# Moving the gate sigmoids of an output tile to a later step, and cutting the last tile's final steps into halves

## The chip, the cores and the metric

The kernel runs on one core of one Trainium2 chip. The metric is the device time of one launch in microseconds (us). A core has five instruction streams that run in order, each by itself, and meet only at semaphores: TensorE (PE in the profile, with its weight loads under PEld), VectorE (DVE), ScalarE (ACT), GpSimd (POOL) and SyncE (SP), which here only issues DMA transfers. Sixteen DMA engines move the data between HBM and SBUF.

## The reference

The program computes one layer of a streaming encoder for 2048 new frames of one stream and for 16 frames of each of 8 running streams (the sample, 128 rows in all, with caches of 512 past frames each). With width 1024, per row:

```
h        = rms_norm(x) * (1 + scale) + shift                 # scale, shift, gate from c @ w_ada + b_ada
qa ka va za qb kb vb zb ga gb = split(h @ w_in)              # 4 x 512, 4 x 512, 2 x 1024 columns
oa       = (softmax1 - lam * softmax2) @ va                  # differential attention, 4 heads
ob       = stick_breaking(qb, kb) @ vb                       # 8 heads
ya       = (rms_norm(oa) * silu(za)) @ w_branch_a
yb       = (ob * silu(zb)) @ w_branch_b
x        = x + gate * ((sigmoid(ga) * ya + sigmoid(gb) * yb) @ w_out)
y        = rms_norm(x) * final_g
```

The outputs are y for all rows and the keys and values ka, va, kb, vb of all new rows. The change lies in the last four lines: in where sigmoid(ga) and sigmoid(gb) are computed, and in the last addition, the norm and the store of y for one of the tiles.

## The kernel before

Rows are worked in 17 tiles of 128: 16 tiles of the prompt (0 to 15) and one for the sample (16). Float32 accuracy comes from float16 matmuls on a high part and a low part of each operand, so every product is three matmuls, and each operand is cut into two halves by a scaled copy (ACT, line 290) and a subtraction (DVE, line 295).

The phases before the last write to HBM, for every tile, the attention results (o_d), the z columns (z_d) and the 2048 gate columns before their sigmoid (g_d). The last phase, lines 1255 on, turns these into y. Two streams of work share it.

The first stream goes through the tiles in the order 0 to 14, 16, 15 (the list `tiles`); the very last is thus tile 15 of the prompt, and the sample is the one before it. A tile passes through these steps:

- `inputs(t)`, lines 1144 to 1179: SP loads o, z and two gate buffers of 128 x 1024 (line 1152); ACT takes the sigmoid of z, DVE and POOL form u = o * silu(z); then two ACT instructions take the sigmoid of the gate buffers in place (line 1167, recorded at line 119, the helper `act`); u is squared and summed (line 272), scaled and split (290, 295).
- `turned(st)`: PE transposes the two halves of u (line 1141) and ACT copies each result out of PSUM (line 1142).
- `branches(st)`: four groups of 12 matmuls (line 1289), each followed on DVE by a product with a gate (line 1291), a sum (1294) and the split into y16 (1295 on ACT, 1296 on DVE).
- `turned_y(st)`: the same transposes and copies for y (lines 1141, 1142).
- `output(t, st, box)`: loads x (line 1311), two groups of 24 matmuls (line 1318), each followed by a product with the adaLN gate (line 1322 on DVE for the prompt, lines 1324 and 1325 for the sample) and the addition to x on POOL (line 1326).
- `normed_rows(t, box)`: squares of x (ACT, line 272), the reciprocal root (ten tiny DVE instructions, lines 253 to 264), the scaling (line 1334) and the store (line 1335).

In round n the loop emits the branches of the n-th tile, the inputs of tile n + 2, the transposing of u of tile n + 1, the norm of tile n - 2, the output of tile n - 1 and the transposing of y of the n-th tile. Four gate buffers serve two tiles at a time, so the gates of tile n + 2 can be loaded only when the branches of tile n have used the buffers (line 1296 or 1291 on DVE).

The second stream is the attention of the sample rows against the caches, in eight units, spread over the first 13 rounds: cache loads (line 728), their cuts (k16c, v16c at lines 290 and 295), transposes made by the DMA engines (lines 735 and 570), scores (line 753), softmax or stick-breaking with sigmoids and exponentials through `act`, and products with the values (line 784, copied out at line 787).

Within a round the pieces are sorted by their share of the round's cost (`interleave`). The order on each engine is then fixed at compile time by a scheduler that goes by its own estimate of durations and readiness. One constraint is written by hand: all instructions made with `act` (sigmoids and exponentials) keep the order in which the program emits them, since a change between the two functions costs a table load on ACT.

Of the kernel before, what the change touches and what calls it, by code (L numbers as in the profile page):

```python
# [16 lines left out]
F32 = mybir.dt.float32  # L17
# [3 lines left out]
AF = mybir.ActivationFunctionType  # L21
ALU = mybir.AluOpType
# [3 lines left out]
P = 128  # L26
D = 1024
# [82 lines left out]
def layer_kernel(ctx: ExitStack, tc: tile.TileContext, a: dict):  # L110
    nc = tc.nc
    V, S, G, T = nc.vector, nc.scalar, nc.gpsimd, nc.tensor
    load = nc.sync.dma_start
# [3 lines left out]
    def act(**kw):  # L117

        i = S.activation(**kw)  # L119
        if last_table[0] is not None:  # L120
            tc.add_manual_dep(i.ins, last_table[0].ins.name, NOSYNC, reason="table order")
        last_table[0] = i
        return i
# [30 lines left out]
    def y_rows(t):  # L154
        return y_p[t * P : (t + 1) * P, :] if t < NT else y_s
# [92 lines left out]
    def rsqrt_one(sums, width, pool, name):  # L248

        c = tiny.tile([P, 4], F32, tag="r1", name="r1")  # L250
        q, t, w = c[:, 0:1], c[:, 1:2], c[:, 2:3]
        i = c[:, 3:4].bitcast(I32)
        V.tensor_scalar(out=q, in0=sums, scalar1=1.0 / width, scalar2=EPS, op0=ALU.mult, op1=ALU.add)
        V.tensor_scalar(out=i, in0=q.bitcast(I32), scalar1=1, scalar2=None, op0=ALU.logical_shift_right)
        y = pool.tile([P, 1], I32, tag=name, name=name)
        V.tensor_scalar(out=y, in0=i, scalar1=-1.0, scalar2=1597463007.0, op0=ALU.mult, op1=ALU.add)
        y = y.bitcast(F32)
        V.scalar_tensor_tensor(out=t, in0=y, scalar=y, in1=q, op0=ALU.mult, op1=ALU.mult)
        V.tensor_scalar(out=w, in0=t, scalar1=0.375, scalar2=-1.25, op0=ALU.mult, op1=ALU.add)
        V.tensor_scalar(out=w, in0=w, scalar1=t, scalar2=1.875, op0=ALU.mult, op1=ALU.add)  # L260
        V.tensor_tensor(out=y, in0=y, in1=w, op=ALU.mult)
        V.scalar_tensor_tensor(out=t, in0=y, scalar=y, in1=q, op0=ALU.mult, op1=ALU.mult)
        V.tensor_scalar(out=w, in0=t, scalar1=-0.5, scalar2=1.5, op0=ALU.mult, op1=ALU.add)
        V.tensor_tensor(out=y, in0=y, in1=w, op=ALU.mult)
        return y

    def sum_squares(src, n, dst, width=1024, scale=1.0):

        for i in range(0, n, width):
            junk = tiny.tile([P, width], F16, tag="junk", name="junk", bufs=1)  # L270
            w = min(width, n - i)
            S.activation(out=junk[:, 0:w], in_=src[:, i : i + w], func=AF.Square, scale=scale,
                         accum_out=dst[:, i // width : i // width + 1])
# [870 lines left out]
    def inputs(t):  # L1144

        o, z = hs[0:2]
        load(out=o, in_=o_d[t])
        load(out=z, in_=z_d[t])
        gs = []
        for j in range(2):  # L1150
            gs.append(L["g"][(2 * len(begun) + j) % 4].rearrange("p (b n) -> p b n", b=2))
            load(out=gs[j], in_=g_d[t].rearrange("p (b n) -> p b n", b=2)[:, :, j * 512 : (j + 1) * 512])
        begun.append(t)
        r = L["orms"][:, 4 * t : 4 * t + 4] if t < NT else rsqrt(osums[:, NT, :], 4, P, tiny, "rA")
        for n in range(2):
            c = slice(n * 512, (n + 1) * 512)
            sg = bank("mm")
            act(out=sg, in_=z[:, c], func=AF.Sigmoid)
            G.tensor_tensor(out=o[:, c], in0=o[:, c], in1=z[:, c], op=ALU.mult)
            if n == 1:  # L1160
                V.tensor_tensor(out=o[:, c], in0=o[:, c], in1=sg, op=ALU.mult)
            else:
                for h in range(4):
                    c = slice(h * P, (h + 1) * P)
                    V.scalar_tensor_tensor(out=o[:, c], in0=sg[:, c], scalar=r[:, h : h + 1], in1=o[:, c], op0=ALU.mult, op1=ALU.mult)
        for g in gs:
            act(out=g, in_=g, func=AF.Sigmoid)

        sq = tiny.tile([P, 2], F32, tag="usq", name="usq")
        sum_squares(o, D, sq[:, 0:1])  # L1170
        V.tensor_tensor(out=sq[:, 1:2], in0=sq[:, 0:1], in1=L["wsq"], op=ALU.mult)
        sc = scales(sq, unit, "suy", 2)
        u16 = hs[2].bitcast(F16).rearrange("p (f n) -> p f n", f=2)
        split(u16[:, 0, :], u16[:, 1, :], o, sc[:, 0:1], S)

        f = unit.tile([P, 2], F32, tag="fuy", name="fuy", bufs=4)
        V.tensor_scalar(out=f[:, 0:1], in0=sc[:, 2:3], scalar1=sc[:, 1:2], scalar2=L["s"][0][:, 1:2], op0=ALU.mult, op1=ALU.mult)
        V.tensor_tensor(out=f[:, 1:2], in0=sc[:, 3:4], in1=L["s"][1][:, 1:2], op=ALU.mult)
        return dict(u16=u16, u=L["u"][len(begun) % 2], f=f, g=gs)

    def turned(st):

        st["u"] = st["u"].bitcast(F16).rearrange("p (k n) -> p k n", n=P)
        for half in range(2):
            transposed(st["u16"], st["u"], half)
# [69 lines left out]
    with ExitStack() as c2:  # L1255
# [50 lines left out]
        def output(t, st, box):  # L1306

            def half(j):
                if j == 0:
                    box["x"] = s2.tile([P, D], F32, tag="x", name="x2", bufs=2)  # L1310
                    load(out=box["x"], in_=x_rows(t))
                x = box["x"]
                c = slice(j * 512, (j + 1) * 512)
                po = bank("o")
                n = 0
                for yi, wi in ((0, 0), (0, 1), (1, 0)):
                    for k in range(KT):
                        T.matmul(po, st["y"][:, yi * 8 + k, :], wo[j * 4 + k // 2][:, wi, k % 2, :], start=(n == 0), stop=(n == 3 * KT - 1))  # L1318
                        n += 1
                m = s2.tile([P, 512], F32, tag="sg", name="m", bufs=2)  # L1320
                if t < NT:
                    V.scalar_tensor_tensor(out=m, in0=po, scalar=st["f"][:, 1:2], in1=gate[:, c], op0=ALU.mult, op1=ALU.mult)
                else:
                    S.activation(out=m, in_=po, func=AF.Identity, scale=st["f"][:, 1:2])
                    V.tensor_tensor(out=m, in0=m, in1=gate_rows(1, j), op=ALU.mult)
                G.tensor_tensor(out=x[:, c], in0=m, in1=x[:, c], op=ALU.add)
            return [(5.2, lambda j=j: half(j)) for j in range(2)]

        def normed_rows(t, box):
            x = box["x"]  # L1330
            acc = tiny.tile([P, 1], F32, tag="facc", name="facc")
            sum_squares(x, D, acc)
            r = rsqrt_one(acc, D, tiny, "rF")
            V.scalar_tensor_tensor(out=x, in0=x, scalar=r, in1=fg, op0=ALU.mult, op1=ALU.mult)
            load(out=y_rows(t), in_=x)

        qpad = res.tile([P, 4, NB, 32], F16, name="qpad")
        G.memset(qpad, 0.0)
# [62 lines left out]
```

## Time and profile before

| what | value |
|---|---|
| time, median of 3 runs | 2353.01 us (2352.11 to 2354.78) |
| time of the profiled execution | 2352.26 us |
| span of the profiled execution | 2350.5 us |
| mean granted TensorE clock | 0.965 of full speed |
| busy: PE / DVE / ACT / POOL | 2124.5 / 1729.8 / 1635.9 / 687.0 us |
| DMA transfers | 453.74 MB, mean 193 GB/s |
| first matmul of the last phase's branches (line 1289) | 1824.06 us |

The profiled execution took 1.8 us more than its span, and 0.75 us less than the median of the timed runs. A line of a timeline gives the start, the duration, the engine, the line of the kernel, the operation, output <- input, and in square brackets the idle time of that engine just before with what ended it. Names of buffers are reused: wb and wa are 128 x 1024 buffers that hold gates, u, y or weights in this phase.

### The profile page before, as it was taken

What the parts mean: (1) busy time and instruction counts of PE and PEld (TensorE: products, weight loads), DVE (VectorE), ACT (ScalarE), POOL (GpSimd) and SP (SyncE); (2) the same over time, 40 slices, a digit from 0 to 9 for tenths busy, and PEclk for the clock granted to TensorE, in tenths of its full rate; (3) what the DMA queues carried; (4) which work ended last, traced back from release to release, by engine and by line L of the source; (5) the groups of instructions that cost most, each with busy time, mean ns of one, the idle gap of its engine ahead of it and who ended that gap; (6) DMA issues with size and microseconds to landing.
All of it is one profiled execution on the core that took longest, in us unless ns stands there. A gap on an engine that the chain in (4) does not pass through costs nothing. (4 is left out here: it accounts for less than half of the span.)

```text
span 2350.5 us, 42534 instructions
## 1 busy us (share of the span) xinstructions
PE 2124.5 (90%) x15272; PEld 1147.0 (49%) x15272; DVE 1729.8 (74%) x3604; ACT 1635.9 (70%) x3148; POOL 687.0 (29%) x563
## 2 busy tenths in 40 slices
PE   5898898998999899899999989999995789889998
PEld 3554454444555444445554544555553344445453
DVE  4847865779775567988666798867678777878763
ACT  4557777777786777778677787866677666666541
POOL 1533012345310233632023364203334222222221
PEclk8999999999999999999999999999997899999999
DMA  9766669887795898878678796866677999998621
GB/s 336 254 203 175 158 137 252 196 195 158 188 238 134 192 222 195 174 171 197 137 178 204 170 196 171 203 150 162 151 170 166 290 254 255 282 238 239 178 100 55
DMA packets 843572, 453.74 MB, mean 193 GB/s; under 512 B 538234, under 2 KB 786346, under 8 KB 842848
## 3 DMA queue, kind: packets, MB, share of 16 engines
q1 hardware_dynamic: 842412, 450.63, 77.2%
q8 instruction: 119, 1.95, 0.3%
q14 instruction: 93, 0.76, 0.1%
q10 hardware_dynamic: 948, 0.39, 0.1%
HBM read 249.80 MB, written 73.44 MB: 138 GB/s over the span
## 5 line engine op out<-in xcount | busy, mean ns | idle before, releaser
L612 POOL TENSOR_TENSOR sc_p<-sc_p,sc_n 128x127 f32<-128x127 f32 (+7 forms) x192 | 311.3, 1625 | 885.5 <-DVE sc_n L606 870.5
L427 PE MATMUL ps_mm<-wb,hs 128*128 128x512 f16 x1632 | 413.4, 380 | 5.0 <-DMA hs<-hT_d 3.2
L427 PEld LDWEIGHTS <-hs 128*128 128x128 f16 x3120 | 273.8, 99 | 252.3 <-issue 12.5
L427 PE MATMUL ps_mm<-wa,hs 128*128 128x512 f16 x1488 | 378.4, 385 | 3.4 <-DVE v L295 2.4
L606 DVE TENSOR_TENSOR_SCAN sc_n<-ps_s,sc_n,zero_t 128x512 f32<-128x512 f32 x192 | 245.3, 1278 | 75.6 <-ACT ps_s L119 72.5
L629 PE MATMUL ps_s<-k,qst 128*128 128x512 f16 (+3 forms) x640 | 225.7, 354 | 47.2 <-DVE sc_n L606 33.7
L563 DVE TENSOR_TENSOR sc_n<-sc_p,sc_n 128x128 f16<-128x128 f32 (+7 forms) x192 | 219.9, 1150 | 51.3 <-ACT sc_n L562 50.8
L494 PEld LDWEIGHTS <-hs 128*128 128x128 f16 x1632 | 154.8, 98 | 182.9 <-DVE qst L522 7.8
L119 ACT ACTIVATE sc_p<-ps_s,usc 128x512 f32<-128x512 f32 (+3 forms) x320 | 203.7, 636 | 44.9 <-PE ps_s L630 34.7
L630 PE MATMUL ps_s<-k,qst 128*128 128x512 f16 (+3 forms) x640 | 225.6, 354 | 0.0
L681 PE MATMUL ps_o<-v,wt 128*128 128x128 f16 x1088 | 175.3, 226 | 36.3 <-DMA wt<-sc_n 36.2
L562 ACT CAST sc_n<-sc_p 128x128 f16<-128x128 f32 (+7 forms) x192 | 154.5, 808 | 65.7 <-POOL sc_p L612 65.0
L494 PE MATMUL ps_t<-wb,hs 128*128 128x512 f16 x816 | 193.5, 381 | 7.0 <-DVE qst L522 6.9
L119 ACT ACTIVATE ps_s<-ps_s,usc 128x512 f32<-128x512 f32 (+3 forms) x328 | 198.6, 606 | 0.0
L494 PE MATMUL ps_t<-wa,hs 128*128 128x512 f16 x816 | 192.1, 380 | 1.7 <-ACT qst L522 1.7
L1318 PE MATMUL ps_o<-wo,wb 128*128 128x512 f16 x816 | 188.6, 386 | 0.7 <-ACT wb L1142 0.7
L682 PE MATMUL ps_o<-v,wt 128*128 128x64 f16 x1088 | 160.1, 198 | 0.0
L681 PEld LDWEIGHTS <-wt 128*128 128x128 f16 x1088 | 106.3, 102 | 104.6 <-DMA wt<-sc_n 48.2
L606 DVE TENSOR_TENSOR_SCAN sc_n<-ps_s,zero_t 128x128 f32<-128x128 f32 (+3 forms) x128 | 104.3, 815 | 48.4 <-ACT ps_s L119 46.3
L548 DVE TENSOR_SCALAR_CACHE_REDUCE sc_p<-ps_s,usc 128x512 f32<-128x512 f32 (+3 forms) x160 | 106.1, 664 | 42.3 <-PE ps_s L630 27.2
L682 PEld LDWEIGHTS <-wt 128*128 128x128 f16 x1088 | 103.9, 101 | 56.3 <-issue 1.9
L548 DVE TENSOR_SCALAR_CACHE_REDUCE sc_n<-ps_s,usc 128x512 f32<-128x512 f32 (+3 forms) x160 | 106.2, 664 | 31.5 <-PE ps_s L630 13.7
(345 smaller groups left out, 4478.0 us busy)
## 6 DMA issues: line engine op xcount, KB each, us to landing
hs<-hT_d SPq DMA_DIRECT2D x130, 512.0 KB, 4.5
g_d<-gt SPq DMA_DIRECT2D x68, 256.0 KB, 4.2
wb<-g_d SPq DMA_DIRECT2D x26, 512.0 KB, 5.7
out_dram<-pr SPq DMA_DIRECT2D x204, 64.0 KB, 2.1
z_d<-pr SPq DMA_DIRECT2D x136, 64.0 KB, 1.8
o_d<-o SPq DMA_DIRECT2D x136, 64.0 KB, 2.4
hs<-z_d SPq DMA_DIRECT2D x17, 512.0 KB, 5.0
hs<-o_d SPq DMA_DIRECT2D x17, 512.0 KB, 6.4
```

Source lines behind the costliest of these rows:

```text
L119: i = S.activation(**kw)
L427: T.matmul(box["p"], box["h"][:, hi, k, :], U["w"][k][:, wi, :], start=(n == 0), stop=(n == 3 * KT - 1))
L494: T.matmul(box["g"][:, 0:gw], box["h"][:, hi, k, :], U["wg"][k // per][:, k % per, wi, :], start=(j == 0), stop=(j == 3 * KT - 1))
L548: V.tensor_scalar(out=dst[:, lo : lo + n], in0=p[:, 0:n], scalar1=sc_pos, scalar2=None, op0=ALU.mult, op1=ALU.max, accum_out=job["mx"][:, ...
L563: V.tensor_tensor(out=lo, in0=src, in1=hi, op=ALU.subtract)
L606: V.tensor_tensor_scan(out=dst[:, lo : lo + n][:, ::-1], data0=src[:, 0:n][:, ::-1], data1=zero_t[:, 0:1].to_broadcast([P, n]), initial=fi ...
L612: G.tensor_tensor(out=p[:, 0:m], in0=p[:, 0:m], in1=n[:, 1 : m + 1], op=ALU.mult)
L629: T.matmul(p[:, 0:n], qst[:, c, :], kk[:, c, 0:n], start=True, stop=False)
L630: T.matmul(p[:, 0:n], qst[:, 2 + c, :], kk[:, c, 0:n], start=False, stop=not diag)
L681: T.matmul(po[:, c * P : (c + 1) * P], wt[:, wj, :], vt[:, c, :, :], start=first, stop=False)
L682: T.matmul(po[:, c * P : c * P + 64], wt[:, nb + wj, :], vt[:, c, 0, :], start=False, stop=last)
L1318: T.matmul(po, st["y"][:, yi * 8 + k, :], wo[j * 4 + k // 2][:, wi, k % 2, :], start=(n == 0), stop=(n == 3 * KT - 1))
```

## The change

Two things. First, the two gate sigmoids leave the end of the first half of `inputs` and are emitted at the beginning of `turned`, for the same tile. For the tiles that the main loop prepares this is one round later: `inputs` of tile n + 2 is emitted in round n, `turned` of that tile in round n + 1. Second, for the last tile alone, the two additions to x go to DVE instead of POOL; the squares are summed in two halves of 512 columns into two columns of `acc`, which a DVE reduction (`add_up`, line 279) adds; and scaling and store are done for columns 0 to 511 and then for 512 to 1023, with two stores of 256 KB instead of one of 512 KB.

```diff
@@ inputs
-        for g in gs:
-            act(out=g, in_=g, func=AF.Sigmoid)
@@ turned
+        for g in st["g"]:
+            act(out=g, in_=g, func=AF.Sigmoid)
         st["u"] = st["u"].bitcast(F16).rearrange("p (k n) -> p k n", n=P)
         for half in range(2):
             transposed(st["u16"], st["u"], half)
@@ output
-                G.tensor_tensor(out=x[:, c], in0=m, in1=x[:, c], op=ALU.add)
+                (V if t == tiles[-1] else G).tensor_tensor(out=x[:, c], in0=m, in1=x[:, c], op=ALU.add)
@@ normed_rows
+            if t != tiles[-1]:
                 acc = tiny.tile([P, 1], F32, tag="facc", name="facc")
                 sum_squares(x, D, acc)
                 r = rsqrt_one(acc, D, tiny, "rF")
                 V.scalar_tensor_tensor(out=x, in0=x, scalar=r, in1=fg, op0=ALU.mult, op1=ALU.mult)
                 load(out=y_rows(t), in_=x)
+                return
+
+            acc = tiny.tile([P, 2], F32, tag="usq", name="usq")
+            sum_squares(x, D, acc, 512)
+            r = rsqrt_one(add_up(acc, 2), D, tiny, "rF")
+            for j in range(2):
+                c = slice(j * 512, (j + 1) * 512)
+                V.scalar_tensor_tensor(out=x[:, c], in0=x[:, c], scalar=r, in1=fg[:, c], op0=ALU.mult, op1=ALU.mult)
+                load(out=y_rows(t)[:, c], in_=x[:, c])
```

More of the change, by code (lines that the diff above doesn't have):

```diff
@@ L1330, in normed_rows @@
             x = box["x"]
[L1331 to L1335, printed above, removed]
+            if t != tiles[-1]:
+                acc = tiny.tile([P, 1], F32, tag="facc", name="facc")
+                sum_squares(x, D, acc)
+                r = rsqrt_one(acc, D, tiny, "rF")
+                V.scalar_tensor_tensor(out=x, in0=x, scalar=r, in1=fg, op0=ALU.mult, op1=ALU.mult)
+                load(out=y_rows(t), in_=x)
+                return
[6 more added lines that the diff above has]
+                load(out=y_rows(t)[:, c], in_=x[:, c])
         qpad = res.tile([P, 4, NB, 32], F16, name="qpad")
```

## The prediction, made before the changed kernel ran

> **What bounds the kernel now.** I read the chain that ended last, then busy time by stage, then what ACT waits for in the stage that the change touches. The chain by line, as shares of the whole span:
>
> ```profile
> PE ps_o L1318 3%; PE ps_mm L1289 2%; DMA wb<-g_d 1%; DMA dwt<-dsc 0%; DVE v16c L295 0%; DMA dc<-in_cache_a_k_dram 0%; PE ps_s L1141 0%; DMA dks<-k16c 0%; PE ps_t L784 0%; ACT v16c L290 0%; DVE wb L1291 0%; DMA dc<-in_cache_b_v_dram 0%; DMA dc<-in_cache_b_k_dram 0%; DMA wa<-g_d 0%; DVE wa L1296 0%
> ```
>
> Its two largest parts are matmuls of the last phase, the third the wait for a gate load (g_d), which only the gate sigmoids have. Next, the last phase in four stages. Columns after the window: PE, PEld, DVE, ACT and POOL busy us with instruction counts, granted clock, DMA share, GB/s.
>
> ```profile
> 1860.00:2210.00 350.00, 313.77 (x2731) 163.43 (x2729) 277.91 (x569) 234.11 (x335) 79.56 (x52) 0.96 0.97 253
> 2210.00:2340.00 130.00, 129.26 (x817) 63.72 (x815) 69.57 (x159) 50.12 (x70) 21.91 (x17) 0.98 0.24 84
> 2340.00:2351.00 11.00, 0.11 (x1) 0.00 (x0) 6.27 (x17) 1.15 (x2) 1.26 (x1) 0.72 0.23 95
> ```
>
> From 2210 to 2340 PE is busy 129.26 of 130.00 us: its order alone sets the length, and what ACT does there is worth nothing. From 1860 to 2210 nothing is full but DMA (0.97): PE has 350 - 313.8 = 36.2 us free. After 2340 a tail of small steps runs out. So the first part of the change can pay only in the middle stage, the second only in the tail. In the middle stage ACT waits for (us in all, times, longest):
>
> ```profile
> ACT wb L119 <- DMA wb<-g_d: 26.7, 13, 4.9
> ACT k16c L290 <- DMA dc<-in_cache_a_k_dram: 17.6, 10, 3.8
> ACT k16c L290 <- DMA dc<-in_cache_b_k_dram: 13.5, 9, 3.3
> ```
>
> The gate sigmoids are the largest group, but casts that wait for the caches (17.6 + 13.5 = 31.1 us) stand in the same queue.
>
> **Part 1: the sigmoids move.** Nothing is added or removed: 34 sigmoids of 1.06 us, the table loads and all g_d loads stay. Emission is a round later, but the scheduler decides the order. In the compiled order on ACT, of the sigmoids of the middle stage that waited, these eight now stand later, behind work that is ready:
>
> ```profile
> 1956.88 1.06 ACT L119 ACTIVATE wb<-wb 128x1024 f32<-128x1024 f32 x1 [3.04 <-DMA wb<-g_d]
> 1979.89 1.06 ACT L119 ACTIVATE wb<-wb 128x1024 f32<-128x1024 f32 x1 [0.38 <-DMA wb<-g_d]
> 1988.29 1.06 ACT L119 ACTIVATE wb<-wb 128x1024 f32<-128x1024 f32 x1 [3.10 <-DMA wb<-g_d]
> 2039.54 1.06 ACT L119 ACTIVATE wb<-wb 128x1024 f32<-128x1024 f32 x1 [1.38 <-DMA wb<-g_d]
> 2051.37 1.06 ACT L119 ACTIVATE wb<-wb 128x1024 f32<-128x1024 f32 x1 [0.27 <-DMA wb<-g_d]
> 2072.22 1.06 ACT L119 ACTIVATE wa<-wa 128x1024 f32<-128x1024 f32 x1 [0.24 <-DMA wa<-g_d]
> 2086.16 1.06 ACT L119 ACTIVATE wb<-wb 128x1024 f32<-128x1024 f32 x1 [2.32 <-DMA wb<-g_d]
> 2145.48 1.06 ACT L119 ACTIVATE wb<-wb 128x1024 f32<-128x1024 f32 x1 [3.03 <-DMA wb<-g_d]
> ```
>
> Their waits add up to 3.04 + 0.38 + 3.10 + 1.38 + 0.27 + 0.24 + 2.32 + 3.03 = 13.8 us. Four others keep their neighbours, and with them their waits (first and last of the four):
>
> ```profile
> 2105.50 1.06 ACT L119 ACTIVATE wb<-wb 128x1024 f32<-128x1024 f32 x1 [1.10 <-DMA wb<-g_d]
> 2179.96 1.06 ACT L119 ACTIVATE wb<-wb 128x1024 f32<-128x1024 f32 x1 [4.86 <-DMA wb<-g_d]
> ```
>
> So the change does half of what its words say: about 13 us of gate waits stay. From 2190 on the ACT order is the old one but for neighbours that swap. The loads themselves are released by DVE at the same points, and no DMA is moved by hand; on SP the compiled order differs by a place or two.
>
> What ACT gains counts only where PE stands still for it. These are PE's gaps that the moved instructions, or the order that comes with them, can touch, and the pace of the matmuls behind a gap and elsewhere:
>
> ```profile
> 1991.28 0.40 PE L753 MATMUL ps_s<-dks,qpad 128*32 128x512 f16 x3 [1.93 <-ACT o L658]
> 1994.71 1.91 PE L1289 MATMUL ps_mm<-wa,wb 128*128 128x512 f16 x4
> 2015.58 0.61 PE L1141 MATMUL ps_s<-id,wa 128*128 128x128 f16 x8 [2.14 <-ACT wa L1142]
> 2044.38 0.48 PE L796 MATMUL ps_t<-ident,ot 128*128 128x128 f32 x1 [4.06 <-ACT ot L787]
> 2046.19 5.91 PE L1318 MATMUL ps_o<-wo,wb 128*128 128x512 f16 x23
> 2052.02 1.05 PE L753 MATMUL ps_s<-dks,qpad 128*32 128x512 f16 x16
> 2044.79 1.47 PE L753 MATMUL ps_s<-dks,qpad 128*32 128x512 f16 x12
> 2080.73 0.74 PE L784 MATMUL ps_t<-dwt,v16c 128*128 128x16 f16 x24 [2.66 <-ACT ot L787]
> 2108.70 0.52 PE L784 MATMUL ps_t<-dwt,v16c 128*64 128x16 f16 x12 [1.86 <-DMA dwt<-dsc]
> 2111.84 1.67 PE L784 MATMUL ps_t<-dwt,v16c 128*64 128x16 f16 x36 [2.10 <-DMA dwt<-dsc]
> 2207.47 0.52 PE L784 MATMUL ps_t<-dwt,v16c 128*64 128x16 f16 x12 [3.24 <-DMA dwt<-dsc]
> 2224.30 5.29 PE ps_o L1318 x24
> ```
>
> - 2044.38: PE waits 4.06 us for `ot`. Ahead of it on ACT stood the sigmoid at 2039.54, with 1.38 of waiting and 1.06 of work; it now stands behind `ot`. Gain 2.4.
> - 2080.73: of the 2.66, the sigmoid at 2072.22 (0.24 + 1.06) stood ahead of the square that feeds u. Gain 1.3.
> - 1991.28: the sigmoid at 1988.29 stood ahead, but so does a cast of a cache, which itself had to wait for its DMA. Nothing gained.
> - 2015.58: a loss. In the new order two sigmoids more stand in the full stretch of ACT ahead of the copy that PE waits for (one square leaves the stretch and one cast enters it, which I let cancel): 2 x 1.06 = 2.1 lost.
> - 2108.70 and 2111.84 (3.96 together) and 2207.47 (3.24): waits for transposed scores. The new PE order puts nine output matmuls more in front of the first two and four branch matmuls more in front of the last: at 5.29 / 24 = 0.22 us each, 2.0 and 0.9 of these gaps would be filled.
> - Slow clock: behind the gap of 4.06, 23 matmuls take 5.91 and twelve of line 753 take 1.47; at the pace of 2224.30 and 2052.02 that would be 5.07 and 0.79, so the gap cost another 1.5.
>
> The last three sums, 2.0 + 0.9 + 1.5 = 4.4, hang on order and clock rather than on a step that I can follow, and I take half, 2.2. The Trainium skill (TensorE: Matmul & The Clock Gate, "What's actually happening") says that the clock halves after an idle window of about 3.4 us; by that, a gap cut from 4.06 to 1.7 would cost no clock, and the whole 1.5 would come back. The trace does not bear it out: behind the gap of 1.93 at 1991.28, four matmuls take 1.91 against 4 x 0.22, twice the usual time, so short gaps lose the clock too.
>
> Middle stage: -2.4 - 1.3 + 2.1 - 2.2 = -3.8 us. Bounds: ACT can give back no more than its 13.8, and the stage moves its bytes in no less than the 0.97 x 350 = 339.5 us that DMA is busy, so at best -10.5. The other end is 10 moved sigmoids (two that had no wait move as well) that all run in front of something late: 10 x 1.06 = +10.6 if every one is paid, about +6 if half are and the gap at 2015.58 grows. Cover: the u copies behind the sigmoids in `turned` have a round's slack; without it each pair costs its 2.1 us. A late sigmoid would stop line 1291 on DVE and with it the PSUM bank that PE fills next; the sigmoids stand many matmuls ahead of that in the new order, so I put it at nothing.
>
> **Part 2: the last tile.** The tail of before:
>
> ```profile
> 2340.22 0.75 DVE L1322 SCALAR_TENSOR_TENSOR m<-ps_o,fuy,gate 128x512 f32<-128x512 f32 x1 [0.20 <-PE ps_o L1318]
> 2341.05 1.26 POOL L1326 TENSOR_TENSOR x<-m,x 128x512 f32<-128x512 f32 x1 [2.42 <-DVE m L1322]
> 2341.32 1.01 DVE L264 TENSOR_TENSOR rF<-rF,r 128x1 f32<-128x1 f32 x1
> 2342.34 1.06 ACT L272 ACTIVATE junk<-x 128x1024 f16<-128x1024 f32 x1 [3.77 <-POOL x L1326]
> 2342.36 1.28 DVE L1334 SCALAR_TENSOR_TENSOR x<-x,rF,gt 128x1024 f32<-128x1024 f32 x1
> 2343.56 0.15 DVE L253 TENSOR_SCALAR r<-facc 128x1 f32<-128x1 f32 x1
> 2345.70 1.28 DVE L1334 SCALAR_TENSOR_TENSOR x<-x,rF,gt 128x1024 f32<-128x1024 f32 x1
> ...
> L1294 DVE TENSOR_TENSOR wb<-wb 128x512 f32<-128x512 f32 x8 | 5.5, 691 | 0.1
> ...
> out_dram<-x SPq DMA_DIRECT2D x17, 512.0 KB, 2.9
> ...
> out_dram<-pr SPq DMA_DIRECT2D x204, 64.0 KB, 2.1
> ```
>
> On its own path the last tile gains: a DVE addition takes 0.69 (line 1294) against 1.26 on POOL, and half a square instead of a whole one saves some 0.5. But DVE is the late one here: the scaling of the sample tile (1.28 at 2342.36) stands in its queue ahead of the last tile's norm, and the old norm began at 2343.56, as that ended. In the new compiled order the addition and two tiny steps come before that scaling, so it starts at about 2340.97 + 0.69 + 3 x 0.19 = 2342.2 (line 264 is no longer held for 1.01 beside POOL's addition) and ends at 2343.5. The new reduction costs about 0.2, so the norm starts at 2343.65, 0.1 later than before. The chain of ten steps is unchanged (2345.70 - 2343.56 = 2.1), the two half scalings need 2 x 0.7 instead of 1.28: done at 2347.2 against 2346.98, 0.2 late. The last store is 256 KB: between 2.1 us for 64 KB and 2.9 for 512 KB, by their line 2.45, so 0.45 less; SP issues the first half meanwhile. Sum -0.2; I take -0.5 with the ends -1.4 (the sample's scaling starts before the addition) and +0.4 (the store no shorter). The Trainium skill (Perfetto Trace Analysis, "Optimizing Scalar/DVE Operations") warns that POOL and DVE share a read port, so that moving work between them may not help; the trace agrees in the 1.01 of line 264 beside POOL's addition. By that warning the tail would be worth 0.
>
> **Sum.** -3.8 - 0.5 = -4.3 us. The profiled execution took 2352.26, so 2347.96; it lies 0.75 under the median of the timed runs, and for a median I expect 2353.01 - 4.3 = 2348.7. A measurement of this kernel tells about 0.2%, 4.7 us, from no change, so the forecast lies just on that line.
>
> **The rivals.**
>
> - Partial gain (forecast), own range 2344 to 2352. For it: the two gaps at 2044 and 2080 have the moved instruction right ahead of PE's releaser. Against it: few gaps carry it.
> - Covered: DMA takes the time up. At a share of 0.97, a cast that no longer queues behind a sigmoid finds its cache not there yet (31.1 us of such waits). Then only the tail is left: 2352.5.
> - The waits come back whole: ACT's casts free the cache buffers earlier, SP issues earlier, and the 10.5 us in which DMA idles fill up: 2353.01 - 10.5 - 0.5 = 2342. For it: the dips of DMA lie in this stage and the chain holds the gate loads. Against it: four long gate waits stay.
> - Slower: sigmoids that ran in ACT's idle time now run in its full stretches. Three pairs stand right behind the two table loads of the softmax, two more in the stretch before 2015.58, all ahead of copies out of PSUM. It decides once more than about four of the ten moved sigmoids stand before a copy that PE waits for (4 x 1.06 = 4.2, the gain). Price +6: 2359. Against it: in the stage as a whole ACT is busy 234 of 350 us.
>
> **How the numbers follow.** Partial gain 0.46, half of it beyond the line; covered 0.19; whole 0.15; slower 0.20. Faster by over 0.2%: 0.23 + 0.15 = 0.38. Within: 0.23 + 0.19 = 0.42. Slower: 0.20. The range leaves out the outer half of the whole gain and of the slower case: 2341.5 to 2358.
>
> **What would show it.** ACT's wait for g_d in the middle stage falls from 26.7 to about 13 us; PE's gaps before `ot` at the places of 2044 and 2080 shrink by 2.4 and 1.3; the gap before the second y or u transpose at the place of 2015 grows by about 2; the PE-bound stage stays near 130 us; from the last matmul to the end of the span stays within 1 us of 2350.5 - 2340.1 = 10.4. It would be wrong if the new orders open other gaps for the transposes of the caches (line 753 waiting on dks), which no row of before can price.

## The result, and the profile after

The changed kernel is slower: a median of 2360.59 us against 2352.81 us for the kernel before, 14 runs of each, ratio 1.0029 with a 95% interval of 1.0017 to 1.0041. That is some 6.8 us (4.0 to 9.6) the wrong way, beyond the upper end of the range, 2358.0. (The ratio is estimated from the runs, so it isn't quite the quotient of the two medians; all times below that come from a comparison are worked out from such ratios.) Ratios go by the fast runs, which leaves out one run in all: 5546.95 us, of the kernel "between the z sigmoids" below. The profiled execution took 2357.31 us with a span of 2355.2.

The busy time by stage, after the change (columns as in the prediction: window, PE, PEld, DVE, ACT, POOL, granted clock, DMA share, GB/s):

```profile
1854.00:2215.00 361.00, 316.05 (x2700) 163.86 (x2699) 277.39 (x573) 233.50 (x335) 75.15 (x52) 0.95 0.97 244
2215.00:2345.00 130.00, 128.85 (x847) 64.38 (x846) 70.65 (x158) 51.04 (x72) 21.16 (x17) 0.99 0.26 86
```

The stage in which PE never pauses is 130 us long, as before. The middle stage has grown from 350 to 361 us, with nearly the same work in it (31 matmuls fewer), DMA as busy as before (0.97) and ACT no busier (233.5 us against 234.1). So the loss lies there. From the first matmul of the branches to the last of the output, 515.6 us became 526.7; of what comes after it, below.

What ACT waits for in that stage and just before it, after the change (us in all, times, longest):

```profile
ACT k16c L290 <- DMA dc<-in_cache_b_k_dram: 26.7, 11, 4.3
ACT k16c L290 <- DMA dc<-in_cache_a_k_dram: 23.6, 8, 5.4
ACT wb L119 <- DMA wb<-g_d: 16.5, 6, 6.8
```

The gate waits fell by 10 us, from 26.7 to 16.5, and the waits for the keys of the caches rose by 19, from 13.5 + 17.6 to 26.7 + 23.6. ACT stands idle in the stage no less than before (350 - 234.1 = 115.9 us then, 361 - 233.5 = 127.5 now); it waits for something else.

PE's gaps after the change: the answers to the places that the prediction named, as far as there still are gaps, and four that it didn't name (1914.78, 1980.43, 2000.00 and 2185.86):

```profile
1914.78 0.71 PE L1141 MATMUL ps_s<-id,wa 128*128 128x128 f16 x5 [3.46 <-DVE dsc L606]
1980.43 0.79 PE L784 MATMUL ps_t<-dwt,v16c 128*128 128x16 f16 x24 [4.61 <-DMA dwt<-dsc]
2000.00 0.33 PE L796 MATMUL ps_t<-ident,ot 128*128 128x128 f32 x1 [1.93 <-ACT ot L787]
2082.86 0.79 PE L784 MATMUL ps_t<-dwt,v16c 128*128 128x16 f16 x24 [2.66 <-ACT ot L787]
2111.67 0.52 PE L784 MATMUL ps_t<-dwt,v16c 128*64 128x16 f16 x12 [1.28 <-DMA dwt<-dsc]
2113.12 1.05 PE L784 MATMUL ps_t<-dwt,v16c 128*64 128x16 f16 x35 [0.93 <-DMA dwt<-dsc]
2185.86 0.77 PE L784 MATMUL ps_t<-dwt,v16c 128*128 128x16 f16 x24 [3.38 <-ACT ot L787]
2214.34 0.52 PE L784 MATMUL ps_t<-dwt,v16c 128*64 128x16 f16 x12 [1.64 <-DMA dwt<-dsc]
```

The gap of 4.06 us before `ot` has gone, but PE's waits for `ot` in the whole phase rose from 8.3 to 10.2 us: some gaps shrank, others opened. And since the scheduler had ordered all engines anew, the two profiles can't be laid side by side instruction by instruction. Telling the sigmoids from the new order was therefore the first question for the chip.

### The profile page after: what moved, and what is told of

It reads as the page before. It is cut to its first block, busy times and chain, and to the rows that moved or that the text cites. A ratio compares the mean times of both kernels' runs of the same rounds, so it can differ in the third digit from the quotient of the medians.

```text
span 2355.2 us, 42529 instructions
## 1 busy us (share of the span) xinstructions
PE 2116.6 (90%) x15272; PEld 1142.3 (49%) x15272; DVE 1730.8 (73%) x3608; ACT 1633.4 (69%) x3150; POOL 680.4 (29%) x561
## 5 line engine op out<-in xcount | busy, mean ns | idle before, releaser
L427 PE MATMUL ps_mm<-wa,hs 128*128 128x512 f16 x1488 | 371.9, 380 | 3.7 <-DVE nm L576 2.4
```

The lines of the kernel that those rows point to most:

```text
L427: T.matmul(box["p"], box["h"][:, hi, k, :], U["w"][k][:, wi, :], start=(n == 0), stop=(n == 3 * KT - 1))
```

## The experiments

Three theories at the start. ORDER: the scheduler's new order makes the loss. PLACE: the sigmoids themselves do, because where they stand now they hold up other work of ACT. COVERED: nothing that ACT gains in this stage reaches PE, since its next wait takes it up.

To separate them, some kernels have the order of the last phase fixed: on each engine, every instruction of it but the gate sigmoids is tied behind its predecessor in the compiled order of another kernel, by an edge that orders and does not wait. Only the sigmoids then change places.

Each comparison below is with runs of the kernel before on the same chip (their median: 2347.87 us for the first four kernels, 2351.33 for the next four, 2346.77 for the last four). The last column is the length of the last phase in the one profiled execution, from the start of the first matmul of the branches to that of the last matmul of the output; it is 515.6 us in the kernel before and 526.7 in the changed one.

| kernel | median us | ratio to before, 95% interval | last phase us |
|---|---|---|---|
| tail alone | 2350.10 | 1.0005 (0.9995 to 1.0015) | 516.6 |
| sigmoids alone | 2357.17 | 1.0028 (1.0013 to 1.0043) | 528.0 |
| new place, old order | 2352.56 | 1.0022 (1.0009 to 1.0034) | 526.9 |
| old place, new order | 2351.48 | 1.0012 (1.0001 to 1.0024) | 516.0 |
| no gate sigmoids | 2350.21 | 0.9995 (0.9981 to 1.0008) | 512.4 |
| a second pair, old place | 2359.84 | 1.0037 (1.0023 to 1.0050) | 521.3 |
| a second pair, new place | 2363.01 | 1.0048 (1.0031 to 1.0064) | 534.5 |
| between the z sigmoids | 2351.99 | 0.9999 (0.9985 to 1.0012) | 516.8 |
| six pairs moved | 2353.25 | 1.0025 (1.0013 to 1.0036) | 524.3 |
| the other pairs moved | 2346.82 | 1.0003 (0.9991 to 1.0016) | 514.4 |
| between, and the tail | 2349.03 | 1.0011 (1.0001 to 1.0021) | 519.2 |
| small gate loads | 2344.01 | 0.9986 (0.9974 to 0.9998) | 510.1 |

**The two parts apart.** The kernel before with the second part of the change alone, and the changed kernel with the last tile as it was:

```diff
 tail alone: in the changed kernel
-        for g in st["g"]:
-            act(out=g, in_=g, func=AF.Sigmoid)      # back to inputs()
 sigmoids alone: in the changed kernel
-                (V if t == tiles[-1] else G).tensor_tensor(out=x[:, c], in0=m, in1=x[:, c], op=ALU.add)
+                G.tensor_tensor(out=x[:, c], in0=m, in1=x[:, c], op=ALU.add)
...
```

> The last tile in halves, the sigmoids at their old place. Every engine has the old order up to the last rows of DVE. All theories: the tail's share of the change alone, -0.5 us (-1.4 to +0.4), which is too little for the time to tell from no change (0.2% of it are 4.7 us). In the profile: last matmul to span end near 9.9 us, 10.4 before. If this kernel came out 5 us or more slower, the loss would be the tail's, against both theories below.

> The sigmoids moved, the last tile whole as before. The orders of all engines are those of the changed kernel up to the tail. All theories put the loss here: slower than before by 5 to 9 us (ratio 1.002 to 1.004).

The tail alone can't be told from no change; the sigmoids alone have the whole loss, 2347.87 x 0.0028 = 6.6 us.

**Place against order.** Two kernels complete a square whose other corners are the kernel before and the changed one:

```diff
 new place, old order: sigmoids in turned(); old place, new order: sigmoids in inputs()
+        for engine, runs in FIXED_ORDER.items():
+            numbers = [k for at, n in runs for k in range(at, at + n)]
+            for k, m in zip(numbers, numbers[1:]):
+                tc.add_manual_dep(mine[engine][m], mine[engine][k].name, NOSYNC, reason="fixed order")
```

> The sigmoids moved, and every other instruction of the last phase held, engine by engine, in the order that the kernel before has; the tail as before. Theory ORDER (the loss is made by the scheduler, which decides all orders anew when the sigmoids move): no loss, and what the moved sigmoids are worth by themselves shows, 0 to -4 us against before (ratio 0.998 to 1.000). Theory PLACE (the moved sigmoids stand in ScalarE's full stretches, ahead of copies and casts that others wait for): the loss stays, +5 to +9 us (1.002 to 1.004). Theory COVERED (this stage goes at the pace of its transfers, ScalarE only waits for other things): within 2 us of before, with ScalarE's waits for g_d down by some 10 us and its waits for the caches up by as much.

> The other corner: the sigmoids at their old place, every other instruction of the last phase held in the order of the changed kernel, the last tile in halves. Theory ORDER: as slow as the changed kernel or slower, +5 to +11 us against before (1.002 to 1.005). Theory PLACE: the time of before, within 2 us. Theory COVERED says nothing of it by itself.

With the old order on every engine, moving the sigmoids costs 5.2 us (2.1 to 8.0), and the last phase is 11.3 us longer in the profile, as much as in the changed kernel. With the new order and the sigmoids at their old place the phase is 516.0 us long, within half a microsecond of before; the timed runs give that corner +2.8 us (0.2 to 5.6), tail included. The two intervals overlap, so by time alone a share for the order is not excluded, and a kernel further below, with another order that the scheduler made, shows 2.6 us as well. In the profile ORDER falls as the main cause, and PLACE stands; the six pairs below test it again, in time.

These two profiles have the same order, so they can be read against each other. Here is ACT around the moved pair that stood at 1942.23 and 1956.88 (the second is in the prediction, with its wait of 3.04 us). The kernel before:

```profile
1958.88 1.13 ACT L290 ACTIVATE k16c<-dc,s_c 128x1024 f16<-128x1024 f32 x1
...
1960.93 1.28 ACT L119 ACT_TABLE_LOAD   x1
1962.22 0.83 ACT L119 ACTIVATE dsc<-dsc,nm 128x640 f32<-128x640 f32 x1
...
1967.60 0.83 ACT L290 ACTIVATE dsc<-dsc,r 128x640 f16<-128x640 f32 x1
...
1968.96 1.28 ACT L119 ACT_TABLE_LOAD   x1
1970.26 0.60 ACT L119 ACTIVATE ps_mm<-hs 128x512 f32<-128x512 f32 x1
1973.15 0.60 ACT L119 ACTIVATE ps_mm<-hs 128x512 f32<-128x512 f32 x1 [2.29 <-DVE hs L1165]
```

And the kernel with the sigmoids moved and all else in the same order (its line numbers are 95 to 98 higher: L387 is line 290, L1239 is 1142):

```profile
1958.68 1.15 ACT L387 ACTIVATE k16c<-dc,s_c 128x1024 f16<-128x1024 f32 x1 [3.10 <-DMA dc<-in_cache_b_k_dram]
...
1960.74 1.28 ACT L214 ACT_TABLE_LOAD   x1
1962.04 0.83 ACT L214 ACTIVATE dsc<-dsc,nm 128x640 f32<-128x640 f32 x1
...
1963.79 1.28 ACT L214 ACT_TABLE_LOAD   x1
1965.08 1.06 ACT L214 ACTIVATE wa<-wa 128x1024 f32<-128x1024 f32 x1
1966.05 1.04 ACT L214 ACTIVATE wb<-wb 128x1024 f32<-128x1024 f32 x1
1966.99 0.99 ACT L1239 COPY wb<-ps_s 128x1024 f16<-128x1024 f16 x1
...
1970.73 0.84 ACT L387 ACTIVATE dsc<-dsc,r 128x640 f16<-128x640 f32 x1
...
1974.80 0.60 ACT L214 ACTIVATE ps_mm<-hs 128x512 f32<-128x512 f32 x1 [2.22 <-DVE hs L1262]
```

The reader is to see two things. First, the wait of 3.04 us for the gate is gone, and in its place the cast of k16c waits 3.10 us for its cache: before, that load had come while the sigmoid waited and worked, so the sigmoid cost nothing there. Second, the pair now stands between the exponentials and the copies, in a stretch in which ACT has no pause. It brings its table load along: before, that load came after the stretch, ahead of z sigmoids that then waited 2.29 us for DVE. From the first exponential to the end of the dsc cast it was 1968.43 - 1962.22 = 6.2 us, and is now 1971.57 - 1962.04 = 9.5: longer by 3.3, which are the 1.28 of the table load and the two sigmoids. The Trainium skill (ScalarE: Activation LUTs, "What ACT_TABLE_LOAD costs") has 1283 ns for the load, and the trace agrees; the drain of about 1380 ns that the section adds to every switch does not show here, for the sigmoid begins at 1965.08, as the load that began at 1963.79 ends.

The dsc cast makes the softmax weights that DVE splits and the DMA engines transpose into dwt, and the products with the values wait for them. What held DVE was not that cast, though, but the cast of k16c in the same stretch: it too begins 3.1 us later (1967.88 against 1964.75), DVE waits 0.89 us for it and comes 1.6 us later to the split of dsc, when the dsc cast has been done for 0.6. The kernel before, then the one with the sigmoids moved:

```profile
1970.55 0.87 DVE L295 SCALAR_TENSOR_TENSOR dsc<-dsc,r 128x640 f16<-128x640 f32 x1
```

```profile
1969.07 1.28 DVE L392 SCALAR_TENSOR_TENSOR k16c<-dc,s_c,k16c 128x1024 f16<-128x1024 f32 x1 [0.89 <-ACT k16c L387]
...
1972.19 0.88 DVE L392 SCALAR_TENSOR_TENSOR dsc<-dsc,r 128x640 f16<-128x640 f32 x1
```

The transpose into dwt is then issued at 1974.0 instead of 1972.3. PE in the same kernel:

```profile
1877.83 0.56 PE L1238 MATMUL ps_s<-id,wa 128*128 128x128 f16 x7 [1.19 <-ACT wa L1393]
1979.53 0.74 PE L881 MATMUL ps_t<-dwt,v16c 128*128 128x16 f16 x24 [1.85 <-DMA dwt<-dsc]
1980.13 2.36 PE L1416 MATMUL ps_o<-wo,wb 128*128 128x512 f16 x6
2018.05 1.01 PE L1238 MATMUL ps_s<-id,wa 128*128 128x128 f16 x8 [4.03 <-ACT wa L1239]
2046.17 0.47 PE L893 MATMUL ps_t<-ident,ot 128*128 128x128 f32 x1 [2.89 <-ACT ot L884]
2073.68 0.75 PE L881 MATMUL ps_t<-dwt,v16c 128*128 128x16 f16 x24 [1.24 <-DMA dwt<-dsc]
2085.17 0.74 PE L881 MATMUL ps_t<-dwt,v16c 128*128 128x16 f16 x24 [2.61 <-ACT ot L884]
2177.69 0.47 PE L881 MATMUL ps_t<-dwt,v16c 128*128 128x16 f16 x13 [1.69 <-ACT ot L884]
```

In the kernel before, the matmuls that answer to 1979.53 and 2073.68 began without a gap:

```profile
1978.65 0.75 PE L784 MATMUL ps_t<-dwt,v16c 128*128 128x16 f16 x24
2067.53 1.46 PE L1318 MATMUL ps_o<-wo,wb 128*128 128x512 f16 x6
2068.98 0.74 PE L784 MATMUL ps_t<-dwt,v16c 128*128 128x16 f16 x24
```

So gaps of 1.85 and 1.24 us were opened, one grew from 2.14 to 4.03, one opened at 1877.83 (for the cast of y16, behind the pair at 1873.3), and the one at 2177.69 grew from 0.35, while just behind it two of 1.42 and 1.01 us closed and one of 0.30 grew to 1.47. The gap before `ot` at the place of 2044.38 fell from 4.06 to 2.89. Counted from the first matmul of the branches, the kernel is 4.1 us behind at 1979.53 (1979.53 - 1820.9 against 1978.65 - 1824.1; 2.2 of them before that gap), 7.9 at 2073.68 and 11.3 at the end.

Behind a gap the clock can be lost too: six output matmuls took 2.36 us after the gap of 1.85, where six took 1.46 in the middle of full work. The Trainium skill (TensorE: Matmul & The Clock Gate, "What's actually happening") speaks of an idle window of about 3.4 us; by these rows, half of that was enough here. It isn't always: behind the gap of 2.14 at 2015.58 in the kernel before, eight transposes took 0.61 us, and behind the one of 4.03 here 1.01. So these rows give no threshold. The lost clock is no small part: over the phase PE stands idle 53.9 us here and 47.5 before, which is 6.4 of the 11.3, and is busy 473.1 us against 468.1 with the same matmuls, which is the other 4.9; the granted clock was 0.94 against 0.95. (In the changed kernel it is 9.7 and 1.4 of 11.1.)

**What the gate waits are worth.** The sigmoids are left out altogether, the order held, so that waits and work are both gone:

```diff
-        for g in gs:
-            act(out=g, in_=g, func=AF.Sigmoid)
```

> The sigmoids of the gates are left out (so the output isn't the reference's); their loads stay, and all other instructions of the last phase are held in the order of the kernel before. It takes ScalarE's waits for g_d out and the sigmoids with them, so it bounds from above what moving them could ever win. Theory WAITS COST (the prediction's: a good part of the 26.7 us in which ScalarE waits for g_d reaches TensorE): 4 to 10 us faster (ratio 0.996 to 0.998). Theory FREE TIME (the sigmoids of the kernel before stand in time that ScalarE has to wait through anyway, because the next cast behind them waits for a cache's load): within 3 us of before (0.9987 to 1.0005), with ScalarE's waits for the caches up by 10 us or more.

FREE TIME, within 3 us. All 26.7 us of waiting for g_d and all 34 sigmoids together are worth 1.2 us (a loss of 1.9 to a gain of 4.5). ACT in that kernel, in the same stage:

```profile
1855.00:2205.00 350.00, 317.25 (x2734) 165.22 (x2733) 280.15 (x572) 214.06 (x315) 81.87 (x54) 0.95 0.98 253
```

```profile
ACT k16c L387 <- DMA dc<-in_cache_b_k_dram: 27.2, 12, 5.8
ACT hs L387 <- DVE suy L323: 19.9, 8, 3.9
ACT k16c L387 <- DMA dc<-in_cache_a_k_dram: 18.5, 13, 3.3
```

ACT is busy 20 us less (214.06 against 234.11) and PE only 3.5 us more. The time went into waits for the caches (45.7 us against 31.1) and for DVE, the second row; that row in the kernel before:

```profile
ACT hs L290 <- DVE suy L226: 8.9, 5, 3.3
```

This is COVERED, shown from its other side: with the order held, the waits that the change went after held next to nothing that could be won.

**The same pair twice.** A second sigmoid of the same buffers, behind the first at the old place, or at the new place with the first left where it was; the order is held:

```diff
 old place, in inputs() behind the first pair; new place, at the start of turned()
+        for g in gs:
+            gate_names.add(act(out=g, in_=g, func=AF.Sigmoid).ins.name)
```

> Each tile's gates go through the sigmoid twice (so the output isn't the reference's): the second pair stands right behind the first, at the place of the kernel before; all other instructions of the last phase are held in its order. Theory FREE TIME: the place of the kernel before is cheap, since casts that wait for a cache's load stand behind it: +0 to +4 us for 15 tiles with some 2 us of ScalarE each. Were ScalarE simply short of time wherever the pair stands, it would cost what the next kernel costs.

> The same second pair (again the output isn't the reference's), but at the place to which the change moves it, beside the transposing of u; the first pair stays where the kernel before has it, and all other instructions are held in its order. Six of these pairs come to stand right behind a softmax's exponentials, in front of copies and casts. Theory FREE TIME: this place is not free, +7 to +14 us (1.003 to 1.006), several times the price of the same instructions at the old place. Were the loss of the change only a matter of fewer or other waits for g_d, this kernel would cost as little as the one with the extra pair at the old place.

The new place costs what was expected, 11.3 us (7.3 to 15.0). The old place does not: 8.7 us (5.4 to 11.8) where 0 to 4 were expected. In time the two can't be told apart; in the profile the last phase is 5.7 us longer with the second pair at the old place and 18.9 us with it at the new one. So the old place is free for one pair, and not for two: FREE TIME as I put it went too far. The comparison is weak support for PLACE at best.

**A third place.** The pair goes between the two z sigmoids of the next tile's inputs, behind the full stretch, where ACT waited 2.29 us above:

```diff
             act(out=sg, in_=z[:, c], func=AF.Sigmoid)
+            if n == 0 and L.get("g_before"):
+                gates(L.pop("g_before"))
...
+        L["g_before"] = gs
```

> A third place: the gates of the tile before are put through the sigmoid between the two z sigmoids of the next tile's inputs, where ScalarE waits some 2 us for VectorE, and where the gates have landed long since; all other instructions of the last phase are held in the order of the kernel before. Theory FREE TIME: the waits for g_d go, the casts behind them wait for the caches instead, no copy comes later: within 3 us of before (0.9987 to 1.0013). Theory WAITS COST: 3 us or more faster. A loss as with the changed kernel (+5 us or more) would mean that leaving the old place is what costs, wherever the pair goes.

No loss and no gain can be told from no change, though these sigmoids come later still. Coming late is not what costs; standing in front of the copies and casts of the stretch is.

**Which pairs.** In the fixed-order kernel six pairs stand right behind the activations of the sample's attention, in front of copies and casts. Four of them follow a softmax's exponentials, with a table load in between; two follow the sigmoids of a stick-breaking, without one (the expectations say exponentials of all six). Either these six alone are moved, or all others:

```diff
 six pairs moved; "not in" for the other pairs
+        moved = len(begun) - 1 in {2, 5, 6, 8, 9, 11}
+        if not moved:
+            gates(gs)
...
+        if st["moved"]:
+            gates(st["g"])
```

> Only the gates of the six tiles whose sigmoids come to stand behind a softmax's exponentials (the third, sixth, seventh, ninth, tenth and twelfth to be begun) are moved; the others keep the place of the kernel before, and all other instructions of the last phase are held in its order. Theory FULL STRETCH (each pair that lands behind the exponentials delays the copies and casts behind it by its 2 us and the table load in front of it): the whole loss, +4 to +8 us (ratio 1.0015 to 1.0035), the last phase 8 us or more longer in the profile. If the loss were spread over all moved sigmoids, about half of it.

> The complement: the gates of all other tiles are put through the sigmoid beside the transposing of u, those six at the old place; the rest in the order of the kernel before. Theory FULL STRETCH: within 2 us of before (0.999 to 1.001). A loss of 3 us or more would say that the six pairs are not the cause, or not alone.

The six carry the loss: 5.9 us (3.1 to 8.4), 8.7 us in the profile, against 0.7 us (-2.1 to 3.8) and -1.2 us for all others; on this one chip the medians of the two are 6.4 us apart. Yet it is the six that shed the gate waits; the other pairs have moved little and keep theirs. The six pairs moved:

```profile
ACT k16c L387 <- DMA dc<-in_cache_b_k_dram: 25.1, 12, 4.5
...
ACT wb L214 <- DMA wb<-g_d: 12.9, 4, 4.3
```

The other pairs moved:

```profile
ACT wb L214 <- DMA wb<-g_d: 22.4, 12, 4.3
```

**The best version that the theory offers.** The third place and the halved last tile, with the scheduler free:

```diff
 between the z sigmoids, and
-            sum_squares(x, D, acc)
+            sum_squares(x, D, acc, 512)              # and the rest of the changed tail
```

> The gates between the z sigmoids of the next tile, and the last tile in halves, with the scheduler free to order everything anew: the best version that the theory offers. FULL STRETCH: the time of before within 3 us (0.9985 to 1.0013), so no gain, since the waits for g_d were worth nothing; better than the changed kernel by 4 us or more. If it came out as slow as the changed kernel, the scheduler's new order would matter after all.

It is 2.6 us (0.2 to 4.9) slower than before, within what was expected, and much like the corner with the old place and the new order (2.8): what a new order costs is perhaps that, but no run separates it from the tail. Nothing tried here that still computes the whole output beats the kernel before.

**Transfers taken away instead.** The gates' loads bring an eighth of their bytes, the sigmoids and the order stay:

```diff
-            load(out=gs[j], in_=g_d[t]...[:, :, j * 512 : (j + 1) * 512])
+            m = 512 if len(begun) < 4 else 64
+            load(out=gs[j][:, :, 0:m], in_=g_d[t]...[:, :, j * 512 : j * 512 + m])
```

> From the fifth tile to be begun, the loads of the gates bring 64 of each 512 columns (the gates' other columns hold old data, so the output isn't the reference's); sigmoids and order stay as in the kernel before. It takes the waits for g_d away by taking transfers away instead of sigmoids. Theory PACED BY TRANSFERS (in the stretch from 1860 to 2210 the DMA engines are busy 0.97 of the time, and ScalarE's, VectorE's and the softmax's waits follow from when caches and transposes land): 6 to 20 us faster (0.9915 to 0.9975), where leaving the sigmoids out won nothing that could be measured. If the pace of that stretch is not set by transfers: within 3 us of before, as without sigmoids.

A gain, of 3.3 us (0.5 to 6.1), and so less than the 6 to 20 expected. The DMA share of the stage fell to 0.91 and the phase by 5.5 us. PACED BY TRANSFERS holds in part only: the share of 0.97 was no floor for the stage. And the wait for g_d hardly fell:

```profile
1862.00:2212.00 350.00, 318.80 (x2761) 165.95 (x2760) 280.29 (x583) 236.60 (x340) 80.29 (x54) 0.96 0.91 228
```

```profile
ACT wb L214 <- DMA wb<-g_d: 23.7, 9, 6.6
```

Part of that wait has nothing to do with bytes. The longest one, on SP and on ACT:

```profile
2168.07 3.46 SPq L832 DMA_TRANSPOSE dks<-k16c  x1
2171.63 0.55 SPq L1250 DMA_DIRECT2D wb<-g_d  x1
```

```profile
2173.99 1.06 ACT L214 ACTIVATE wb<-wb 128x1024 f32<-128x1024 f32 x1 [6.64 <-DMA wb<-g_d]
```

ACT stood idle from 2167.35, but SP issued the load only at 2171.63, when it had issued a transpose for 3.46 us. Of the 23.7 us, 7.6 passed before the load was issued (2.3, 1.0 and 4.3 at 1956.64, 1986.01 and 2173.99), of the 26.7 in the kernel before only 0.5. From the issue on ACT waited 16.1 us, against 26.2: smaller loads did shorten that part.

## Why the prediction was wrong

- **ACT's wait for g_d.** Forecast to fall from 26.7 to about 13; it fell to 16.5. (Both are sums over 1824 to 2210 and its like; 1.3 of the 26.7 lie before the middle stage.) The eight sigmoids that were to lose their waits lost them. Of the four that were to keep theirs three did, and their waits grew from 10.8 to 14.0 us.
- **What that is worth.** Here the prediction failed first. It took two gaps at PE as gains because the moved sigmoid stood ahead of PE's releaser. In the same order, the gap at 2044.38 shrank by 1.2, not 2.4, and the one at 2080.73 by 0.05, not 1.3 (2.61 at 2085.17). Even the 1.2 was not won by ACT: counted from the first matmul, `ot` came 5 us later than before, and PE, itself 6 us late, had less to wait for. The next instruction behind the sigmoid took up what it left, and the trace of before had that row, with a wait of its own (first before, then with the sigmoids moved; 1.38 + 1.06 + 0.85 = 3.29 us against 3.35):

```profile
2041.45 1.15 ACT L290 ACTIVATE k16c<-dc,s_c 128x1024 f16<-128x1024 f32 x1 [0.85 <-DMA dc<-in_cache_b_k_dram]
```

```profile
2043.24 1.15 ACT L387 ACTIVATE k16c<-dc,s_c 128x1024 f16<-128x1024 f32 x1 [3.35 <-DMA dc<-in_cache_b_k_dram]
```

The bound "ACT can give back no more than its 13.8" was no bound of use: the kernel without gate sigmoids shows that all of it is worth 1.2 us, with an upper end of 4.5. The rival Covered had this mechanism, at a chance of 0.19.
- **The pair in front of 2015.58.** Forecast +2.1; in the same order the gap grew from 2.14 to 4.03, by 1.9. So the mechanism and the size hold where the order is the old one, and this term applied to more than one pair. In the changed kernel itself PE nowhere waits for that copy (line 1142 of wa), so at this very place the term was not paid.
- **"Cover: the u copies behind the sigmoids in `turned` have a round's slack; without it each pair costs its 2.1 us."** This is the step that failed most. The sum costed the other pairs in the full stretches at nothing. Whatever slack the u copies have (no run tests them alone), in the same stretch stand the y16 cast, the casts of the caches and the dsc cast, and the first two had none: PE waits for one at 1877.83, DVE for the other at 1969.07. Six pairs cost 5.9 us in time and 8.7 in the profile, 1.0 to 1.5 us a pair, and not all of ACT's delay arrives (at the pair shown, 3.3 us of ACT became 0.89 of waiting at DVE and a gap of 1.85 at PE). The table load that moved with four of the pairs (1.28 us) stood in no term.
- **The order's terms, -2.2.** The three dwt gaps did shrink with the new order, from 3.96 to 2.21 and from 3.24 to 1.64 (forecast by 2.0 and 0.9, of which half was taken). But the corner with only the order new is as long as before (516.0 us), so what these gained was lost at others. A gap that an order fills is no gain until the rest of the order has been counted too. The slow clock went against the change, since there are more gaps, not fewer: PE's busy time over the phase rose by 1.4 us in the changed kernel and by 4.9 in the one with the old order. (The prediction's reading of short gaps set 1.91 us for four matmuls against 4 x 0.22; a row of four in full work takes 1.02 with its last one, so they took 1.9 times as long.)
- **The tail, -0.5.** From the last output matmul's start to the end of the span: 10.8 before, 10.3 after, and 10.3 with the tail alone. Right to a tenth, in part by luck, and invisible in time: the sum itself gave -0.2, and -0.5 was taken. The store took some 0.4 less, as worked out; the steps before it ended 0.1 us earlier, not 0.2 later. The sample tile's scaling was the late one, as said; after the change:

```profile
2347.19 1.28 DVE L1335 SCALAR_TENSOR_TENSOR x<-x,rF,gt 128x1024 f32<-128x1024 f32 x1
...
2350.66 1.42 DVE L1344 SCALAR_TENSOR_TENSOR x<-x,rF,gt 128x512 f32<-128x512 f32 x2
```

- **The doubt that it ended with.** New gaps for the transposes of the caches were not the cause: PE's waits for dks are 6.3 us before and after.
- **The rival Slower.** Place and price were right: sigmoids from ACT's idle time into its full stretches, +6 against 6.8 measured. The price was a rounded half of ten sigmoids, so its nearness is luck in part. Three pairs were counted behind the softmax's table loads; in the trace of the changed kernel they are four. Its condition, a copy that PE waits for, was too narrow: at the pair shown DVE waited for a cast. What spoke against it in the text, "in the stage as a whole ACT is busy 234 of 350 us", is the error in one line: an average over the stage says nothing of a stretch without a pause. And Covered and Slower were treated as alternatives. They are two sides of one thing: where the time that is freed is covered and the time that is taken is not, the sign is decided.

One thing stays open. The profiled executions show a larger loss (8.7 to 12.4 us in the last phase, in four kernels with the six pairs moved) than the timed runs of the same kernels (5.2 to 6.8). Each is one execution, and some are extreme: with the sigmoids alone and with the new place in the old order it was the slowest of its kernel's runs (2361.57 us with a median of 2357.17, 2360.37 with one of 2352.56). In the changed kernel (2357.31, median 2360.59) and with the six pairs (2353.34, median 2353.25) it was not, so this isn't the whole of it. How much the length of the phase varies from one execution to the next was not measured; in five kernels that lost little or nothing in time (before, tail alone, old place with the new order, between the z sigmoids, the other pairs moved) it lies between 514.4 and 516.8 us. It was also not tried to hold the six pairs behind the stretch while leaving them in `turned`; the third place is the nearest to that.

## What to carry to other kernels

Before an instruction is moved out of a wait, look at what stands behind it on its engine: if the next one waits for something that comes no sooner, the wait is worth nothing, and the instruction was free where it stood. Then cost it at its new place by the stretch that it lands in, not by the engine's average: every copy and cast behind it up to the next pause comes later by its length, and by that of a table load that comes with it. Both can be asked of the compiled order and the trace of before: which instruction is next in line, when did its own input land, and where is the next pause.

## What the runs showed of the hardware

- Loads of 64 KB instead of 512 KB landed 3.9 us after their issue in the median (5.7 before). ACT's wait from the issue on fell from 26.2 to 16.1 us, yet its whole wait only from 26.7 to 23.7, since it now stood waiting for 7.6 us before the loads were issued at all. Ahead of the two longest of these stood a DMA transpose, which SP took 3.46 and 4.41 us to issue.
- A gap of 1.85 us at PE was followed by six matmuls that took 2.36 us where full work takes 1.46, so on these six alone it cost half as much again, 0.9 us. A gap of 2.14 us in the kernel before was followed by eight transposes in 0.61 us, where the same eight took 1.01 behind a gap of 4.03. The length of a gap alone did not decide.
- Two orders of PE that differ in 1869 of the 3657 places of the last phase's list gave phases of 515.6 and 516.0 us. In the profile, where six pairs of sigmoids stand (8.7 us) mattered more than the order of everything else.
